# A two-layer token mixer on one core: three weight groups instead of two in the opening of layer 1, and the last convolution moved behind two low parts

## The chip, the core and the metric

One core of a Trainium2 chip runs the whole kernel. The metric is the time of one execution on the device, in microseconds (us). For the kernel before, three timed runs gave 1090.76, 1093.69 and 1093.97 us, median 1093.69. One further execution was recorded by the hardware profiler; all rows shown here are from it.

## The reference

Two layers work on 1024 tokens of width 1024 in fp32. Layer 0 (Fourier mixing beside differential attention, then a gate and an output projection) is not touched by the change, apart from the end of its output projection, where work for layer 1 begins. Layer 1 is a gated short convolution:

```
h = modulate(x, norm_g[1], shift, scale)       # RMS norm per token, then scale and shift
bg, cg, xt, g = split(h @ odd_w_in, 4)         # 1024 -> 4096
u = cg * xt
conv = sum(conv_w[t] * up[:, t:t+n] for t in range(3))   # up is u padded by one token
y = (bg * conv * silu(g)) @ odd_w_out          # 1024 -> 1024
x = x + gate * y
```

## The kernel before

All products are fp32 work on TensorE, done as three matmuls: each factor is split into a high part (a rounded cast) and a low part (value minus high part), and high x high, high x low and low x high are added. The high part is a cast on ScalarE (L61 for weights, L1506 for activations), the low part a subtraction on VectorE or GpSimd (L62, L1309 and L1310 for weights, L1510 for activations).

Layer 1's two projections go by Strassen's scheme in Winograd's form: a block product of 2 x 2 takes seven products of blocks instead of eight. The weights come in 20 groups `g`. Groups 0 to 15 are the input projection, an even `g` giving a tile of `u`, the odd one after it the gated `y`; groups 16 to 19 are the output projection. Each group has seven products `(g, p)`, p = 1 to 7. A product is four `quarters` of three matmuls, 128x512 each, on lines L657 to L659; it needs

- a weight part, made by `wop(g, p)` (L1300) from the raw tiles that `wload(g)` (L1288) fetches by two transfers on SP's queue. p = 1, 2, 3, 4, 6, 7 read a quarter of the raw tiles; p = 5 reads a sum, and `wpart` (L634) makes it and two other sums in place, on GpSimd. A fourth sum, `a_hi -= a_lo`, may be made only once the parts 2 and 5 have read the old values. The argument `held` keeps it for later; `later` makes the cast at once and returns the subtraction as a closure.
- an activation part `B[p]` of four tiles. B1 and B2 are the two token halves. B5, B6, B7, B4 and B3 are sums and differences of them. In layer 1's opening they are built in place from `x1`: `scaled` and `t1` (L1499, L1502) for B5, `shifted` and `t2` (L1516, L1523) for B6, `t3` (by L1502) for B7, `t4` (L1531) for B4, and plain halves for B3, each with `hi` (L1506) and `lo` (L1510).

The products of a group add up in PSUM banks of three kinds: X takes p = 1, 6, 7 and 4 (three buffers), Y p = 5 and 3 (two), Z p = 2 (one). X is read between its products: after (g,1), (g,6), (g,7) and (g,4), while the next of them adds to it.

After a product, `finish1` (L1338) takes what is ready out of the banks: p = 1, 6 and 7 copy X on ScalarE (L1354, L1360, L1363), p = 2 adds Z (L1356), p = 7 adds Y (L1364), p = 4 multiplies by X (L1366), p = 3 adds Y and multiplies (L1371, L1374). After p = 3 of a `u` group the three-tap convolution `conv` runs on VectorE (L1386, L1389). A gated group has a silu besides and ends in the multiplication with the convolution's result `vv`. `finish2` (L1419) does the like for the output projection.

Layer 1 can't scale its second token half before that half's RMS statistics are there: `stats_mid` and `rows_mid` make token sums on TensorE (L209), a root's argument on VectorE (L216), a power on GpSimd (L218), a diagonal `dg` on VectorE (L220) and a row on TensorE (L228). They stand between matmuls of (0,2) and (1,1).

What sets the order: in the opening (the first twelve products, groups 0 and 1) PE, VectorE, ScalarE and GpSimd follow the order in which the code is written, `manual_schedule`. In the middle, up to (13,7), only PE does, and a scheduler places the rest. From (14,1) on all four do again: this is the seam, where groups 14 and 15 end, the output projection's activation parts are built from `ysd` by `bop` (table `hooks`), and the weight parts of groups 16 and on are made, five products ahead (`LEAD`), with their low parts held one product (`rests`, `due`).

Of the kernel before, what the change touches and what calls it, by code (L numbers as in the profile page):

```python
# [37 lines left out]
def block_kernel(tc, A):  # L38
# [1260 lines left out]
    def wop(g, p, eng=None, later=False, held=None):  # L1299

        pool = wpools[0]
        wpools.append(wpools.pop(0))
        rest = []

        def out(src, e):
            o = pool.tile([P, 2, NB], F32R, name="wop", bufs=4 if pool is wp else 2)
# [3 lines left out]
            rest.append(lambda: e.tensor_tensor(out=o[:, 1, :], in0=src, in1=f32(o[:, 0, :]), op=ALU.subtract))  # L1310
# [138 lines left out]
    for half in range(2):  # L1449
        y0(half)  # L1450
        for f in range(KT):
            if half == 0 or f < KT - 1:
# [8 lines left out]
            if half == 1 and f == KT - 1:
                for q in order[:5]:
                    wop(*q)
                man.__exit__(None, None, None)
                man = tc.manual_schedule(engines=MANUAL)
                man.__enter__()
# [238 lines left out]
```

## Time and profile before

| | before |
|---|---|
| median of three runs | 1093.69 us |
| profiled execution | 1093.98 us, span 1092.2 us, mean granted clock of TensorE 0.981 |
| busy: TensorE, VectorE, ScalarE, GpSimd | 1039.5, 753.0, 481.9, 466.8 us |
| HBM read, written | 105.57 MB, 24.64 MB |
| layer 1's first twenty products | 661.10 to 739.50 us of the span |
| the other products of the input projection up to the seam | 739.50 to 985 us |
| the seam and the start of the output projection | 985 to 1030 us |

A row of the trace reads: start, duration, engine, source line, operation, output<-inputs, shapes, count, and in brackets how long the engine stood idle before it and which instruction released it. A row of stages reads: window, length, busy time and instructions of each engine, granted clock as a share of full speed, share of the DMA engines in use, GB/s. A row of waits reads: matmul and line, released by, idle us in all, count, longest. A row of groups reads: line, engine, operation, tiles, shapes, count | busy us, mean ns | idle us before it.

### The profile page before, as it was taken

What the parts mean: (1) busy time and instruction counts of PE and PEld (TensorE: products, weight loads), DVE (VectorE), ACT (ScalarE), POOL (GpSimd) and SP (SyncE); (2) the same over time, 40 slices, a digit from 0 to 9 for tenths busy, and PEclk for the clock granted to TensorE, in tenths of its full rate; (3) what the DMA queues carried; (4) which work ended last, traced back from release to release, by engine and by line L of the source; (5) the groups of instructions that cost most, each with busy time, mean ns of one, the idle gap of its engine ahead of it and who ended that gap; (6) DMA issues with size and microseconds to landing.
All of it is one profiled execution on the core that took longest, in us unless ns stands there. A gap on an engine that the chain in (4) does not pass through costs nothing.

```text
span 1092.2 us, 14128 instructions
## 1 busy us (share of the span) xinstructions
PE 1039.5 (95%) x5128; PEld 847.3 (78%) x5128; DVE 753.0 (69%) x1093; ACT 481.9 (44%) x876; POOL 466.8 (43%) x398
## 2 busy tenths in 40 slices
PE   6989999999999899999999998899999999998998
PEld 3667888878877698999888886578888888786786
DVE  4599956958786388888853287986545645578953
ACT  4453333313345377777753363633333333344420
POOL 1257115620445147766575445655344354402041
PEclk8999999999999999999999999999999999999999
DMA  9823895353112978161006450121111211202431
GB/s 337 329 97 113 260 367 214 110 166 115 59 44 78 244 185 189 38 163 57 11 20 210 166 189 34 38 77 40 59 58 39 77 40 58 77 20 97 143 126 59
DMA packets 61381, 131.12 MB, mean 120 GB/s; under 512 B 5248, under 2 KB 30208, under 8 KB 58112
## 3 DMA queue, kind: packets, MB, share of 16 engines
q1 hardware_dynamic: 60240, 125.64, 36.7%
q0 software_dynamic: 1072, 4.59, 1.2%
q8 instruction: 40, 0.66, 0.2%
q14 instruction: 29, 0.24, 0.1%
HBM read 105.57 MB, written 24.64 MB: 119 GB/s over the span
## 4 chain that ended last, share of the span: by engine, by line
PE 64%; DVE 20%; POOL 5%; ACT 4%; issue 3%; DMA 3%; SPq 0%; ACTq 0%; POOLq 0%; DVEq 0%
PE psX L657 6%; PE psX L659 6%; PE psX L658 6%; PE ps_av L1075 5%; PE ps_tok L284 3%; PE ps_tok L285 3%; PE ps_tok L286 3%; PE psY L657 3%; PE psY L659 3%; PE psY L658 3%; PE S L1025 3%; PE S L1026 2%; DVE nm L1030 2%; PE ps_t L1065 2%; PE ps_feat L1128 2%
## 5 line engine op out<-in xcount | busy, mean ns | idle before, releaser
L284 PE MATMUL ps_tok<-whi,hhi 128*128 128x512 f32 x288 | 118.5, 412 | 2.5 <-ACT hhi L393 1.5
L285 PE MATMUL ps_tok<-whi,hlo 128*128 128x512 f32 x288 | 115.3, 400 | 3.6 <-DVE hlo L397 3.5
L286 PE MATMUL ps_tok<-wlo,hhi 128*128 128x512 f32 x288 | 114.6, 398 | 0.0
L61 ACT CAST wop<-wraw 128x512 fp32r<-128x512 f32 x118 | 72.5, 620 | 93.4 <-PE ps_feat L1130 27.6
L1030 DVE TENSOR_REDUCE nm<-S 128x1 f32<-128x1280 f32 x64 | 95.2, 1487 | 20.5 <-PE S L1026 18.4
L634 POOL TENSOR_TENSOR s<-wraw 128x512 f32<-128x512 f32 x20 | 27.9, 1395 | 185.3 <-DMA wraw<-in_wodd_dram 118.1
L62 POOL TENSOR_TENSOR wop<-wraw,wop 128x512 fp32r<-128x512 f32 x60 | 83.1, 1388 | 51.5 <-ACT wop L61 51.5
L1041 ACT ACTIVATE p<-S,nm 128x1280 f32<-128x1280 f32 x64 | 85.1, 1330 | 43.2 <-DVE nm L1030 39.4
L657 PE MATMUL psX<-B,wop 128*128 128x512 f32 x240 | 96.7, 403 | 7.5 <-ACT c L1363 3.5
L658 PE MATMUL psX<-B,wop 128*128 128x512 f32 x240 | 96.5, 402 | 1.5 <-POOL B L1510 1.0
L659 PE MATMUL psX<-B,wop 128*128 128x512 f32 x240 | 96.1, 401 | 1.8 <-DVE wop L1310 1.3
L1075 PE MATMUL ps_av<-v,aT 128*128 128x128 f32 x640 | 76.8, 275 | 0.0
L1075 PEld LDWEIGHTS ps_av<-v,aT 128*128 128x128 f32 x640 | 74.2, 192 | 0.2
L285 PEld LDWEIGHTS ps_tok<-whi,hlo 128*128 128x128 f32 x288 | 55.5, 193 | 16.9 <-DVE hlo L397 6.0
L659 PE MATMUL psY<-B,wop 128*128 128x512 f32 x160 | 64.3, 402 | 4.1 <-DVE wop L1310 4.1
L284 PEld LDWEIGHTS ps_tok<-whi,hhi 128*128 128x128 f32 x288 | 55.6, 193 | 16.2 <-issue 2.1
L1052 POOL TENSOR_TENSOR p<-p,cc 128x256 f32<-128x256 f32 x32 | 40.3, 1259 | 63.8 <-DVE cc L1049 44.6
L286 PEld LDWEIGHTS ps_tok<-wlo,hhi 128*128 128x128 f32 x288 | 55.4, 192 | 12.2 <-DVE wlo L172 0.2
L658 PE MATMUL psY<-B,wop 128*128 128x512 f32 x160 | 64.1, 401 | 0.6 <-POOL B L1510 0.3
L657 PE MATMUL psY<-B,wop 128*128 128x512 f32 x160 | 64.0, 400 | 0.0
L657 PEld LDWEIGHTS psX<-B,wop 128*128 128x128 f32 x240 | 45.7, 191 | 21.3 <-ACT c L1363 4.8
L658 PEld LDWEIGHTS psX<-B,wop 128*128 128x128 f32 x240 | 45.7, 191 | 14.3 <-POOL B L1510 2.4
(347 smaller groups left out, 2696.0 us busy)
## 6 DMA issues: line engine op xcount, KB each, us to landing
ada_raw<-in_ada_dram SPq DMA_DIRECT2D x24, 1024.0 KB, 7.6
wraw<-in_wodd_dram SPq DMA_DIRECT2D x32, 512.0 KB, 3.5
wraw<-in_wo_dram SPq DMA_DIRECT2D x24, 512.0 KB, 4.1
wraw<-in_wtok_dram SPq DMA_DIRECT2D x16, 512.0 KB, 5.1
arena<-kd SPq DMA_DIRECT2D x16, 320.0 KB, 9.3
kq<-kd SPq DMA_DIRECT2D x16, 320.0 KB, 10.1
xt<-in_xT_dram SPq DMA_DIRECT2D x16, 256.0 KB, 5.8
xr<-in_xT_dram SPq DMA_DIRECT2D x16, 256.0 KB, 4.0
```

The costliest lines, as they stand in the source:

```text
L61: nc.scalar.copy(out=o[:, 0, :], in_=src)
L62: eng.tensor_tensor(out=o[:, 1, :], in0=src, in1=f32(o[:, 0, :]), op=ALU.subtract)
L284: nc.tensor.matmul(ps, lhsT=hh, rhs=whi, start=k == 0, stop=False)
L285: nc.tensor.matmul(ps, lhsT=hl, rhs=whi, start=False, stop=False)
L286: nc.tensor.matmul(ps, lhsT=hh, rhs=wlo, start=False, stop=k == KT - 1)
L657: nc.tensor.matmul(ps, lhsT=a, rhs=x[k][0], start=start and k == 0, stop=False, skip_group_check=not start)
L658: nc.tensor.matmul(ps, lhsT=a, rhs=x[k][1], start=False, stop=False, skip_group_check=not start)
L659: nc.tensor.matmul(ps, lhsT=b, rhs=x[k][0], start=False, stop=k == 3, skip_group_check=not start)
L1030: nc.vector.tensor_reduce(out=nm, in_=S[m][:, :NKEY], op=ALU.max, axis=AX.X, negate=True)
L1041: nc.scalar.activation(out=p, in_=S[m][:, :NKEY], func=AF.Exp, bias=tiles.pop((i, m, "nm")), accum_out=z)
L1052: nc.gpsimd.tensor_tensor(out=p1[:, ks], in0=p1[:, ks], in1=c.broadcast_to([P, POOLK]), op=ALU.mult)
L1075: nc.tensor.matmul(ps, lhsT=groups[i, k // 4][:, (k % 4) * P:(k % 4 + 1) * P], rhs=v[:, k * P:(k + 1) * P], start=k == 0, stop=k == NK - 1)
```

## The change

In words:

- Groups 0, 1 and 2 open layer 1 together, 17 hand-ordered products and three more, instead of groups 0 and 1 with twelve. `order` now begins with six products from B1 and B2.
- Group 0's raw weights go into `w2` and are loaded half a projection earlier; group 2's go into the buffers of `B3` before `B3` is made; two of `B3`'s four tiles go into `x1` buffers.
- All low parts of the opening are made on VectorE; GpSimd has only the weight sums left there. The casts are taken forward (`later=True`) and the subtractions stand where the code names them. The sums `a_hi -= a_lo` of groups 1 and 2 are held, and run on VectorE after (0,4).
- The token sums stand after the first quarter of (0,2) instead of the second.
- `finish1` of (0,3), (1,3) and (14,3) returns its tail, `last`: the convolution or the multiplication with `vv`. For group 14 the tail stands behind the low parts that are due.
- `y` of groups 11 and 13 lies in `B3` buffers; (1,2) uses a Y buffer and (2,5) a buffer of the pool `pst`.

The core of the diff:

```diff
-    wpools[:] = [wp, wp, wp, wp, w2, w2]
+    wpools[:] = [w2, w2, wp, wp, wp, wp]
...
-                pool = (wp, w2)[g % 2]
-                t = pool.tile([P, KT * P], F32, name="wraw", bufs=2)
+                if g == 2:
+                    t = hB.tile([P, KT * P], F32, name="wraw", tag="B3", bufs=4)
+                else:
+                    t = (w2, wp)[(g + (g > 2)) % 2].tile([P, KT * P], F32, name="wraw", bufs=2)
...
-        if p == 3:
-            rest.append(lambda: wload(g + 2))
+        if p == 3 and g != 2:
+            rest.append(lambda: wload(g + 2 + (g < 2)))
...
-            if gated:
+            def last():
+                if not gated:
+                    return conv(ct, ubuf[ct % 2])
+                if g == 1:
+                    nc.vector.tensor_mul(out=h0, in0=h0, in1=vv[:, 0:NB])
                 nc.vector.tensor_mul(out=h1, in0=h1, in1=vv[:, NB:T])
                 ysd.append(us[g])
-            else:
-                conv(ct, ubuf[ct % 2])
+
+            if g in (0, 1, 14):
+                return last
+            last()
...
-    order = [(0, 1), (0, 2), (1, 1), (1, 2), (0, 5), (1, 5), (0, 6), (1, 6), (0, 7), (1, 7), (0, 4), (0, 3)]
-    for g in range(2, 14):
-        order += [(g, 1), (g - 1, 4), (g, 5), (g - 1, 3), (g, 6), (g, 2), (g, 7)]
+    order = [(0, 1), (0, 2), (1, 1), (1, 2), (2, 1), (2, 2), (0, 5), (1, 5), (2, 5), (0, 6), (1, 6), (0, 7), (1, 7),
+             (0, 4), (1, 4), (0, 3), (1, 3), (2, 6), (2, 7), (2, 4)]
+    NMAN = 17
+    for g in range(3, 14):
+        order += [(g, 1)] + [(g - 1, 4)] * (g > 3) + [(g, 5), (g - 1, 3), (g, 6), (g, 2), (g, 7)]
...
-    product(0, 2, (2, stats_mid))
-    wop(1, 6, G)
+    wop(1, 5, V, held=held)
+    product(0, 2, (1, stats_mid))
...
+    w06 = wop(0, 6, V, True)
+    t2(3), lo(6, 2, V)
+    w16 = wop(1, 6, V, True)
+    w06()
+    lo(6, 3, V)
     product(1, 5)
-    shifted(0), shifted(1), t2(0), shifted(2), t2(1), lo(6, 0, V), lo(6, 1, G), shifted(3), t2(2), t2(3), lo(6, 2, V)
-    lo(6, 3, G)
-    wop(0, 7, G)
-    fin12()
-    t3(0), t3(1), lo(7, 0, V), lo(7, 1, G)
+    product(2, 5)
+    t3(0), w16(), t3(1), lo(7, 0, V), t3(2), lo(7, 1, V), t3(3), lo(7, 2, V)
+    w07 = wop(0, 7, V, True)
+    lo(7, 3, V)
     product(0, 6)
...
     product(0, 4)
-    product(0, 3)
+    for f in held:
+        f()
...
-        product(g, p)
+        tail = product(g, p)
         for f in due:
             f()
+        if tail:
+            tail()
```

How this moves rows, at three places. The rows are instructions in the order in which the engine takes them, with line, operation, output<-inputs and size.

First, VectorE between B6 and B7. Tiles `x1` are the activations that are being turned from one part into the next, `wop` with `wraw` is a weight's low part. Before, where only every second low part is here and GpSimd has the others:

```order
L1510 TENSOR_TENSOR B6_6240<-x1_5513,B6_6240 128x512
L1356 TENSOR_TENSOR y_6161<-y_6161,psZ_6184 128x512
L1502 SCALAR_TENSOR_TENSOR x1_5484<-x1_5484,shift1_90,x1_5593 128x512
L1502 SCALAR_TENSOR_TENSOR x1_5498<-x1_5498,shift1_90,x1_5633 128x512
L1510 TENSOR_TENSOR B7_6253<-x1_5484,B7_6253 128x512
L1502 SCALAR_TENSOR_TENSOR x1_5513<-x1_5513,shift1_90,x1_5673 128x512
L1502 SCALAR_TENSOR_TENSOR x1_5553<-x1_5553,shift1_90,x1_5713 128x512
L1510 TENSOR_TENSOR B7_6274<-x1_5513,B7_6274 128x512
```

And in the changed kernel, from the low part of (0,6) to the first step of B4:

```order
L1312 TENSOR_TENSOR wop_6267<-wraw_5851,wop_6267 128x512
L1531 TENSOR_TENSOR B6_6270<-x1_5553,B6_6270 128x512
L1522 SCALAR_TENSOR_TENSOR x1_5484<-x1_5484,shift1_90,x1_5593 128x512
L1312 TENSOR_TENSOR wop_6273<-wraw_5991,wop_6273 128x512
L1522 SCALAR_TENSOR_TENSOR x1_5498<-x1_5498,shift1_90,x1_5633 128x512
L1531 TENSOR_TENSOR B7_6304<-x1_5484,B7_6304 128x512
L1522 SCALAR_TENSOR_TENSOR x1_5513<-x1_5513,shift1_90,x1_5673 128x512
L1531 TENSOR_TENSOR B7_6308<-x1_5498,B7_6308 128x512
L1522 SCALAR_TENSOR_TENSOR x1_5553<-x1_5553,shift1_90,x1_5713 128x512
L1531 TENSOR_TENSOR B7_6312<-x1_5513,B7_6312 128x512
L1531 TENSOR_TENSOR B7_6316<-x1_5553,B7_6316 128x512
L1552 TENSOR_TENSOR x1_5593<-x1_5593,x1_5484 128x512
```

All four low parts of B7, and the weights' low parts of (0,6) and (1,6), now stand in VectorE's row.

Second, ScalarE at the copy of (2,6), `u` from a bank X (L1360 before, L1366 now). The tiles `wraw_6425` before and `wraw_6434` now are raw weights of group 3, `s1` is a weight sum of p = 5. Before:

```order
L61 CAST wop_6468<-wraw_6425 128x512
L61 CAST wop_6484<-wraw_6305 128x512
L61 CAST wop_6507<-s1_6503 128x512
L1373 ACTIVATE y_6162<-y_6162 128x512
L1360 COPY u_6449<-psX_6436 128x512
L61 CAST wop_6523<-wraw_6303 128x512
L61 CAST wop_6544<-wraw_6425 128x512
L1363 COPY c22_6559<-psX_6436 128x512
```

Now:

```order
L1379 ACTIVATE y_6163<-y_6163 128x512
L61 CAST wop_6499<-wraw_6434 128x512
L61 CAST wop_6538<-s1_6534 128x512
L61 CAST wop_6541<-wraw_6085 128x512
L1366 COPY u_6440<-psX_6197 128x512
L1398 ACTIVATE vv_5454<-u_6106,small_76 128x512 x2
L61 CAST wop_6544<-wraw_6434 128x512
L1369 COPY c22_6559<-psX_6197 128x512
```

The casts of group 3 still stand ahead of the copy, but group 3 is now loaded behind the low part of (1,3), and (2,6) and (2,7) follow each other on PE.

Third, VectorE at the seam: the last convolution (taps of 128x256 and less into `vv`) and the low parts of (16,5), `wop` from `s1`, and (17,1). Before:

```order
L1374 TENSOR_TENSOR u_6449<-u_6449,c22_8286 128x512
L1389 SCALAR_TENSOR_TENSOR vv_5454<-u_6449,small_76,vv_5454 128x256 x2
L1389 SCALAR_TENSOR_TENSOR vv_5454<-u_6449,small_76,vv_5454 128x254 x2
L1389 SCALAR_TENSOR_TENSOR vv_5454<-u_6449,small_76,vv_5454 128x255 x2
L1389 SCALAR_TENSOR_TENSOR vv_5454<-u_6449,small_76,vv_5454 128x254 x2
L1389 SCALAR_TENSOR_TENSOR vv_5454<-u_6449,small_76,vv_5454 128x2 x4
L1310 TENSOR_TENSOR wop_8327<-s1_8323,wop_8327 128x512
L1310 TENSOR_TENSOR wop_8354<-wraw_8318,wop_8354 128x512
L1366 TENSOR_TENSOR y_8150<-y_8150,psX_8137 128x512
```

Now:

```order
L1380 TENSOR_TENSOR u_6440<-u_6440,c22_8286 128x512
L1312 TENSOR_TENSOR wop_8327<-s1_8323,wop_8327 128x512
L1401 SCALAR_TENSOR_TENSOR vv_5454<-u_6440,small_76,vv_5454 128x256 x2
L1401 SCALAR_TENSOR_TENSOR vv_5454<-u_6440,small_76,vv_5454 128x254 x2
L1401 SCALAR_TENSOR_TENSOR vv_5454<-u_6440,small_76,vv_5454 128x255 x2
L1401 SCALAR_TENSOR_TENSOR vv_5454<-u_6440,small_76,vv_5454 128x254 x2
L1401 SCALAR_TENSOR_TENSOR vv_5454<-u_6440,small_76,vv_5454 128x2 x4
L1312 TENSOR_TENSOR wop_8354<-wraw_8318,wop_8354 128x512
L1372 TENSOR_TENSOR y_8150<-y_8150,psX_8137 128x512
```

The low part of (16,5) has passed the convolution; that of (17,1) stands where it stood.

More of the change, by code (lines that the diff above doesn't have):

```diff
@@ L1326, in product @@
         if start:
-            banks[g, bank] = pst.tile([P, NB], F32, name="ps" + bank, tag="t", bufs=2) if (g, p) in ((16, 5), (17, 2)) \
+            banks[g, bank] = pst.tile([P, NB], F32, name="ps" + bank, tag="t", bufs=2) \
+                if (g, p) in ((2, 5), (16, 5), (17, 2)) else acc.tile([P, NB], F32, name="psY", bufs=2) if (g, p) == (1, 2) \
                 else acc.tile([P, NB], F32, name="ps" + bank, bufs={"X": 3, "Y": 2, "Z": 1}[bank])
@@ L1332, in product @@
             return lambda: fin(g, p)
-        fin(g, p)
+        return fin(g, p)
     part22 = {}
@@ L1340, in finish1 @@
         X, Y_, Z = (banks.get((g, i)) for i in "XYZ")
+        if p == 5:
+            return
         if p == 1:
@@ L1344, in finish1 @@
             elif gated:
-                us[g] = halves(xp.tile([P, T], F32, name="y", tag="x1", bufs=KT))
+                us[g] = halves(hB.tile([P, T], F32, name="y", tag="B3", bufs=4) if g in (11, 13) else
+                               xp.tile([P, T], F32, name="y", tag="x1", bufs=KT))
             else:
@@ L1366, in finish1 @@
             nc.vector.tensor_tensor(out=h0, in0=h0, in1=X, op=ALU.mult)
-            if gated:
+            if gated and g > 1:
                 nc.vector.tensor_mul(out=h0, in0=h0, in1=vv[:, 0:NB])
@@ L1453, in block_kernel @@
                 w0next()
+            if half == 1 and f == 2:
+                wload(0)
             if half == 1 and f == KT - 2:
-                wload(0)
                 wload(1)
+                man.__exit__(None, None, None)
+                man = tc.manual_schedule(engines=MANUAL)
+                man.__enter__()
             if pend:
@@ L1460, in block_kernel @@
                 ps = proj_feat2(W[half * KT + f], half)
+            if half == 1 and f == KT - 2:
+                wop(0, 1, nc.vector)
+                wop(0, 2, nc.vector)
             if half == 1 and f == KT - 1:
[L1462 to L1466, printed above, removed]
+                wop(1, 1, nc.vector)
+                wop(0, 5, nc.vector)
             out0(half, f, ps)
@@ L1483, in block_kernel @@
     LEAD = 5
-    wop(1, 5)
+    wload(2)
+    wop(1, 2, nc.vector)
     late = {}
+    held = []
     def stats_mid():
@@ L1535, in block_kernel @@
     product(0, 1)
-    wop(0, 6)
-    product(0, 2, (2, stats_mid))
-    wop(1, 6, G)
+    wop(1, 5, V, held=held)
+    product(0, 2, (1, stats_mid))
+    w21 = wop(2, 1, V, True)
+    w22 = wop(2, 2, V, True)
     product(1, 1, (2, rows_mid))
-    scaled(0), scaled(1), t1(0), scaled(2), t1(1), lo(5, 0, V), lo(5, 1, G), scaled(3), t1(2), t1(3), lo(5, 2, V)
-    lo(5, 3, G)
+    w21()
+    w22()
     fin12 = product(1, 2, later=True)
-    product(0, 5)
-    product(1, 5)
-    shifted(0), shifted(1), t2(0), shifted(2), t2(1), lo(6, 0, V), lo(6, 1, G), shifted(3), t2(2), t2(3), lo(6, 2, V)
@@ L1546, in block_kernel @@
-    lo(6, 3, G)
-    wop(0, 7, G)
-    fin12()
-    t3(0), t3(1), lo(7, 0, V), lo(7, 1, G)
+    w25 = wop(2, 5, V, True, held)
+    scaled(0), scaled(1), t1(0), scaled(2), t1(1), lo(5, 0, V), lo(5, 1, V)
+    fin2 = [product(2, p, later=True) for p in (1, 2)]
+    scaled(3), t1(2), t1(3), lo(5, 2, V), lo(5, 3, V)
+    fin12()
+    w25()
+    product(0, 5)
+    shifted(0), shifted(1), t2(0), shifted(2), t2(1), lo(6, 0, V), lo(6, 1, V), shifted(3), t2(2)
+    w06 = wop(0, 6, V, True)
+    t2(3), lo(6, 2, V)
@@ L1550, in block_kernel @@
+    w16 = wop(1, 6, V, True)
+    w06()
+    lo(6, 3, V)
+    product(1, 5)
+    product(2, 5)
+    t3(0), w16(), t3(1), lo(7, 0, V), t3(2), lo(7, 1, V), t3(3), lo(7, 2, V)
+    w07 = wop(0, 7, V, True)
+    lo(7, 3, V)
     product(0, 6)
-    t3(2), t3(3), lo(7, 2, V), lo(7, 3, G)
-    wop(1, 7, G)
+    t4(0), w07(), t4(1), lo(4, 0, V)
+    w17 = wop(1, 7, V, True)
     product(1, 6)
-    wop(0, 4, G)
-    wop(0, 3, G)
-    t4(0), t4(1), lo(4, 0, V), lo(4, 1, G), t4(2), t4(3), lo(4, 2, V), lo(4, 3, V)
+    t4(2), lo(4, 1, V), t4(3), w17(), lo(4, 2, V)
@@ L1557, in block_kernel @@
+    w04 = wop(0, 4, V, True)
+    lo(4, 3, V)
     product(0, 7)
-    hi(3, 0), hi(3, 1), lo(3, 0, V), lo(3, 1, G), hi(3, 2), hi(3, 3), lo(3, 2, V), lo(3, 3, G)
+    w04()
+    hi(3, 0), hi(3, 1)
+    w14 = wop(1, 4, V, True)
+    lo(3, 0, V), hi(3, 2), lo(3, 1, V), hi(3, 3), w14(), lo(3, 2, V)
     product(1, 7)
-    wop(2, 1)
+    w03 = wop(0, 3, V, True)
+    lo(3, 3, V)
     product(0, 4)
-    product(0, 3)
+    for f in held:
+        f()
+    w03()
+    w13 = wop(1, 3, V, True)
+    for f in fin2:
+        f()
@@ L1563, in block_kernel @@
+    w13()
+    product(1, 4)
+    w26 = wop(2, 6, V, True)
+    w27 = wop(2, 7, V, True)
+    w26()
+    w27()
+    tails = [product(0, 3)]
+    wop(2, 4, V)
+    tails.append(product(1, 3))
+    wop(3, 1, V)
+    product(2, 6)
+    for f in tails:
+        f()
     man.__exit__(None, None, None)
@@ L1573, in block_kernel @@
     for n, (g, p) in enumerate(order):
-        if n < 12:
+        if n <= NMAN:
             continue
```

6 lines of the change are left out of this document (3 added, 3 removed).

## The prediction

> **What bounds the kernel now.** I read the page first, then the busy time by stage, then what TensorE waited for in the stages that lose time, then single rows there.
>
> ```profile
> span 1092.2 us, 14128 instructions
> PE 1039.5 (95%) x5128; PEld 847.3 (78%) x5128; DVE 753.0 (69%) x1093; ACT 481.9 (44%) x876; POOL 466.8 (43%) x398
> ...
> core 0: us, PE busy (x) PEld busy (x) DVE busy (x) ACT busy (x) POOL busy (x), PEclk, DMA share, GB/s
> 661.10:739.50 78.40, 66.62 (x260) 49.36 (x259) 67.88 (x79) 35.09 (x61) 47.81 (x33) 0.93 0.13 44
> 739.50:985.00 245.50, 245.29 (x1052) 196.76 (x1051) 137.20 (x224) 93.93 (x159) 94.44 (x68) 1.00 0.17 54
> 985.00:1030.00 45.00, 38.15 (x148) 29.02 (x147) 42.30 (x67) 20.39 (x37) 8.62 (x6) 0.92 0.29 92
> ```
>
> TensorE is the bound, and the change neither adds nor removes a matmul, so only its idle time and its slowed clock can be won. Between 739.50 and 985 it never rests: nothing is to be had there. Two stages lose time at a clock below 1: the opening of layer 1 (661.10 to 739.50) and the seam to the output projection (985 to 1030). In both VectorE is nearly full, 67.88 of 78.40 and 42.30 of 45.
>
> ```profile
> 661.10 0.40 PE L657 MATMUL psX<-arena,wop 128*128 128x512 f32 x1
> 665.30 0.28 PE L209 MATMUL ps_ss<-ones,x1ss 128*128 128x1 f32 x2
> 667.00 0.48 PE L657 MATMUL psZ<-arena,wop 128*128 128x512 f32 x1
> 673.71 1.44 PE L228 MATMUL ps_r<-dg,ones 128*128 128x512 f32 x2 [3.67 <-DVE dg L220]
> 674.27 1.30 PE L657 MATMUL psX<-arena,wop 128*128 128x512 f32 x1
> 705.64 0.79 PE L657 MATMUL psX<-B,wop 128*128 128x512 f32 x1 [2.46 <-ACT c L1363]
> 707.08 0.63 PE L657 MATMUL psX<-B,wop 128*128 128x512 f32 x1
> 707.51 0.63 PE L658 MATMUL psX<-B,wop 128*128 128x512 f32 x1
> 732.25 0.67 PE L657 MATMUL psX<-B,wop 128*128 128x512 f32 x1 [2.65 <-ACT u L1360]
> 736.70 0.40 PE L657 MATMUL psX<-arena,wop 128*128 128x512 f32 x1
> 739.50 0.40 PE L657 MATMUL psX<-B,wop 128*128 128x512 f32 x1
> 992.96 0.50 PE L657 MATMUL psX<-B,wop 128*128 128x512 f32 x1 [0.84 <-ACT c L1363]
> ```
>
> One product (12 matmuls) takes 739.50 - 736.70 = 2.80 us at full clock. The first twenty products of layer 1 end at 739.50; undisturbed they are 56.0 us, and they took 78.4: 22.4 lost. Of this the token sums (667.00 - 665.30 = 1.7) and the row of statistics (674.27 - 673.71 = 0.6) are work. The other 20.1 are three long waits (3.67, 2.46, 2.65), the matmuls behind each, which start 0.43 apart (707.51 - 707.08) instead of 2.80/12 = 0.23, and small waits for VectorE's and GpSimd's low parts.
>
> **The change in the opening.** Before, twelve products stand against the building of the activation parts; now twenty do. TensorE gets six products from the first two activation parts (six against four) before it needs VectorE's next one, then three, two, two, two, two.
>
> The statistics:
>
> ```profile
> 657.49 1.76 POOL L634 TENSOR_TENSOR s<-wraw 128x512 f32<-128x512 f32 x1 [4.74 <-DMA wraw<-in_wodd_dram]
> 668.93 1.77 DVE L62 TENSOR_TENSOR wop<-wraw,wop 128x512 fp32r<-128x512 f32 x1 [1.30 <-ACT wop L61]
> 670.86 1.02 POOL L218 TENSOR_TENSOR rs<-rs,mhalf 128x4 f32<-128x4 f32 x1 [0.70 <-DVE rs L216]
> 671.91 1.75 DVE L220 TENSOR_TENSOR dg<-cst,rs 128x512 f32<-128x512 f32 x1 [1.13 <-POOL rs L218]
> ```
>
> The token sums ended at 667.0, but a weight's low part (668.93 to 670.7) stood ahead of the root on VectorE. That part hangs on GpSimd's sums, which began at 657.49 with group 0's. In the new order group 0's four sums stand far ahead, among GpSimd's low parts in layer 0's output projection, so group 1's come first and I put that part ready at about 666.5; and the token sums stand three matmuls sooner. My chain: sums end 666.3, root on VectorE 667.2, power 1.0, `dg` 1.75 as now, row 670.5. TensorE has nine and six matmuls (3.5) until 669.9: it waits 0.7, not 3.67. VectorE's first `scaled` comes at 673.0, behind two low parts for group 2, against 675.19.
>
> VectorE's pace (first row: the stretch from the first scaling step to the last `B3` part, VectorE busy and its instructions):
>
> ```profile
> 675.19:710.20 35.01, 34.11 (x38) 0.91 0.09 30
> 675.19 1.41 DVE L1499 SCALAR_TENSOR_TENSOR x<-x,sc,ps_r 128x512 f32<-128x512 f32 x2 [0.94 <-PE ps_r L228]
> 685.98 0.68 DVE L1510 TENSOR_TENSOR B<-x,B 128x512 fp32r<-128x512 f32 x1
> 686.58 0.74 DVE L1499 SCALAR_TENSOR_TENSOR x<-x,sc,ps_r 128x512 f32<-128x512 f32 x1
> 687.24 2.01 DVE L1523 TENSOR_TENSOR x<-x,x 128x512 f32<-128x512 f32 x2
> 706.70 2.99 POOL L1510 TENSOR_TENSOR B<-x,B 128x512 fp32r<-128x512 f32 x2 [1.13 <-ACT B L1506]
> 707.25 3.00 DVE L1510 TENSOR_TENSOR B<-x,B 128x512 fp32r<-128x512 f32 x2
> 685.50 0.73 ACT L1516 ACTIVATE x<-x,shift 128x512 f32<-128x512 f32 x1
> 686.13 0.61 ACT L1506 CAST B<-x 128x512 fp32r<-128x512 f32 x1
> ```
>
> Alone, a low part takes 686.58 - 685.98 = 0.60 and a scaling step 687.24 - 686.58 = 0.66; beside GpSimd two low parts take 3.00. The change takes GpSimd out of this stretch, so VectorE inherits nine low parts of B and five of weights but runs at 0.60 and 0.66. Ends of the change's cost for a low part moved over: 0.60 and 1.50 each; I take 0.60, since GpSimd's queue holds only the sums of groups 2 and 3 now. The two held sums cost VectorE 2 x 0.60 late, where TensorE has work.
>
> The walk along VectorE's queue from 673.0: 26 instructions (12 of 0.66, 14 of 0.60: 16.3) and an estimated 1.5 of gaps for ScalarE's shifts and casts (0.73 and 0.61 each) up to the low part of (0,6): 690.8. Twelve more (7.4) to that of (0,7): 698.2. Six more (3.6) to that of (1,7): 701.8. TensorE reaches (0,5) at 661.1 + 6 x 2.8 + 1.7 + 0.7 + 0.6 = 680.9 and needs the low part of (0,6), its third matmul, at 680.9 + 8.4 + 0.5 = 689.8: it waits 1.1. Two products on, 696.5 against 698.2: 1.7. One product on, 701.1 against 701.8: 0.7. After that VectorE is ahead.
>
> New waits: (2,6), (2,7) and (2,4) now follow each other in one bank, so each copy by ScalarE stands open; the nearest row, the 0.84 wait at 992.96, prices one at 0.9. The first is worse: on ScalarE the copy stands behind the cast of group 3's sum, which needs a load that SP issues behind VectorE's low part of (1,3).
>
> ```profile
> wraw<-in_wodd_dram SPq DMA_DIRECT2D x10, 512.0 KB, 3.6
> ```
>
> I put the issue at 712.2 (third of a burst), the landing at 716.2, GpSimd's sum 1.3, two casts, the copy at 719.6: TensorE, ready at 718.1, waits 1.6. Ends: 0.9, and 5 if the load lands late.
>
> Sum of waits: 0.7 + 1.1 + 1.7 + 0.7 + 1.6 + 0.9 = 6.7. For slowed matmuls behind them the ends are 0.1 each (behind the 0.84 wait the next matmul is late by that) and 1.5 each (2.46: six or seven matmuls, 0.2 each). Three of mine lie at 1.1 to 1.7, nearer the first: 1.0 in all. The twenty products end at 661.1 + 56.0 + 2.3 + 6.7 + 1.0 = 727.1, against 739.5: **12.4 us won**.
>
> The Trainium skill (TensorE: Matmul & The Clock Gate, Part 1) lets the clock fall only after an idle window of about 3.4 us. By it none of my waits would slow a matmul, and the result would be 1.0 lower; the trace disagrees, since waits of 2.46 and 2.65 did.
>
> ```profile
> L62 POOL TENSOR_TENSOR wop<-wraw,wop 128x512 fp32r<-128x512 f32 x26 | 36.1, 1392 | 37.3 <-ACT wop L61 37.3
> ```
>
> Costed at nothing: group 0's four early sums during the output projection of layer 0 (the row is 560 to 661: GpSimd idles 37.3/26 = 1.4 before each low part, so four sums of about 1.3 are caught up within four parts; without that cover TensorE would wait up to 5.2 there); group 2's raw weights in the `B3` buffers; two `B3` parts in `x1` slots, free by then.
>
> **The change at the seam.**
>
> ```profile
> PE psY L659 <- DVE wop L1310: 4.1, 1, 4.1
> PE psX L659 <- DVE wop L1310: 1.3, 2, 0.8
> ...
> 1001.10 4.40 DVE L1389 SCALAR_TENSOR_TENSOR vv<-u,small,vv 128x256 f32<-128x256 f32 x12
> 1005.42 0.69 DVE L1310 TENSOR_TENSOR wop<-s,wop 128x512 fp32r<-128x512 f32 x1
> ...
> 1006.34 1.51 POOL L634 TENSOR_TENSOR s<-wraw 128x512 f32<-128x512 f32 x1 [10.03 <-DVE wop L1310]
> 1009.62 1.28 POOL L634 TENSOR_TENSOR wraw<-s,wraw 128x512 f32<-128x512 f32 x1
> ...
> L1389 DVE SCALAR_TENSOR_TENSOR vv<-u,small,vv 128x254 f32<-128x254 f32 x4 | 4.0, 996 | 0.0
> ```
>
> Only the low part of (16,5) passes the last convolution; that of (17,1) stays behind it. The 4.1 wait goes, and (17,1) waits instead. VectorE is full until its low part of (17,6), the last that TensorE waits for, so its work decides. That frees GpSimd's sums for (17,5) to run beside the convolution (4.4 us, 1006.34 to 1010.9), whose taps then take about 1.0 instead of 4.40/12 (0.48 the large ones): +2.2, less the 1.4 by which the same sums slow VectorE's steps now: about +0.5 with the rest. The last `B3` casts now wait for low parts that read `y` of groups 11 and 13: one gap of 0.8. Ends: -2.6 (the 4.1 and the small waits gone) to +2.5; I take **1.3 lost**.
>
> By the Trainium skill (SBUF — State Buffer, two separate sides) a GpSimd instruction and a VectorE one with two SBUF inputs exclude each other for whole instructions. By that the convolution would grow by all of 4.4 and the time would be 2.2 higher; the rows, 996 ns a tap beside GpSimd, say about half.
>
> **Sum.** 12.4 - 1.3 = 11.1. The profiled execution took 1093.98 outside a span of 1092.2; it gives 1082.9. The median of the runs is 0.3 lower, 1093.69: **1082.6**.
>
> **Rivals.**
> - TensorE bound throughout: VectorE starts and runs a little better, and no low part is late. Then 56.0 + 2.3 and perhaps 1 of waits, about 18 won: 1075 (with the seam's best 1072). For it: my three VectorE waits are under 2 us. Against: VectorE's 54 instructions from `scaled` to the last `B3` part are 33.5 at the bare pace, so a wait of some kind stays.
> - The third group's chain gives half back: the load for group 3, or ScalarE's queue behind the silu of group 1, holds (2,7) for 5 to 6 with the clock behind it, as 2.65 at 732.25 did. Then 5 to 6 won: 1088.
> - Nothing won: after the opening VectorE has two convolutions in a row, TensorE catches up with it and the opening's gain is waited off there: 1091 to 1095. Against it: VectorE is 137.20 of 245.50 in the next stage.
> - Slower: VectorE's slowness isn't GpSimd's doing. From 675.19 to 710.20 it ran 38 instructions in 35.01, 0.92 each. At that pace the 54 take 49.7 instead of 33.5 + 1.5 = 35.0: 14.7 later, against 11.1 won, and with the clock behind the waits 1098. It decides from (35.0 + 11.1)/54 = 0.85 an instruction. Against it: the slow rows all lie beside GpSimd rows.
>
> **How the numbers follow.** The forecast 0.60 (own range 1079.5 to 1086), TensorE bound 0.14, half given back 0.14, nothing won 0.07, slower 0.05. The runs before lie within 0.3% of each other, about what a measurement can tell. Faster by more is 0.60 + 0.14 + 0.14 = 0.88, within it 0.07, slower 0.05. The range 1076 to 1089 leaves out half of the first rival, and of the others nothing won and slower.
>
> **What would show it.** In the profile after: the wait for `dg` under 1.5; no GpSimd row of B; low parts of B at 0.69; the first twenty products in 64 to 69 us; waits for weights' low parts at (0,6) and (0,7), and for ScalarE's copy at (2,7). At the seam: the wait of 4.1 at (17,1) instead of (16,5), taps near 1.0. Wrong would be a wait over 3 us in the opening, or low parts of B still over 1 us.

## The result, and the profile after

The changed kernel takes 1081.25 us, median of three runs (1080.91 to 1082.07), against 1093.69: a ratio of 0.9902, 95% interval 0.9879 to 0.9926, so 1% faster. Run twice more among the experiments, on two chips, it gave 0.9908 (0.9891 to 0.9925) and 0.9913 (0.9899 to 0.9928), 9.5 to 9.8 us under the medians of before there. The forecast was 1082.6.

The profiled execution took 1081.25 outside a span of 1079.4. By stage (window, length, busy time of TensorE, its weight loads, VectorE, ScalarE and GpSimd, then the clock), first of before and then of the changed kernel. The opening of before stands in the prediction, so its rows begin with the stretch from the end of the twentieth product to the start of (14,1); the last row of each is the seam, counted here and below from the start of (14,1), at 952.30 in before, to the start of (18,1):

```profile
739.50:952.30 212.80, 212.80 (x914) 170.94 (x913) 115.86 (x190) 78.46 (x131) 90.57 (x65) 1.00 0.17 55
952.30:1047.72 95.42, 88.36 (x361) 69.07 (x360) 76.83 (x119) 39.49 (x70) 18.95 (x13) 0.96 0.32 103
```

```profile
658.83:722.71 63.88, 59.94 (x259) 46.67 (x258) 58.08 (x86) 34.69 (x61) 15.46 (x11) 1.00 0.13 39
722.71:935.56 212.85, 212.85 (x914) 171.11 (x913) 124.34 (x201) 77.84 (x131) 89.49 (x64) 1.00 0.17 55
935.56:1034.69 99.13, 88.59 (x362) 68.72 (x360) 79.73 (x119) 39.80 (x70) 18.01 (x13) 0.97 0.31 102
```

The reader is to see three differences. The first twenty products take 63.88 instead of 78.40 (14.5 won), at full clock, and GpSimd is busy 15.46 there instead of 47.81. The middle is unchanged. The seam takes 99.13 instead of 95.42 (3.7 lost). A fourth lies ahead of all changed work: layer 1 begins at 658.83 instead of 661.10. 2.27 + 14.52 - 0.05 - 3.71 = 13.0, which is the span's 12.8 but for the last stretch.

What TensorE still waits for in the two stages (released by, idle us in all, count, longest), the opening first, then the seam:

```profile
PE psX L657 <- ACT u L1366: 2.5, 2, 1.3
PE psX L659 <- DVE wop L1312: 0.7, 2, 0.6
PE psX L657 <- ACT c L1369: 0.7, 1, 0.7
...
PE psX L659 <- DVE wop L1312: 7.4, 3, 3.8
PE psY L658 <- DVE B L1259: 1.7, 1, 1.7
PE psX L657 <- ACT c L1369: 0.9, 2, 0.7
PE psZ L659 <- DVE wop L1312: 0.6, 1, 0.6
```

In the opening the longest wait is 1.32, and the wait for `dg` is gone. In the seam the 4.1 has become a 3.8; two waits for weights' low parts have grown, at (16,6) from 0.60 to 2.06 and at (17,6) from 0.75 to 1.51; and one for `B3`, ahead of (16,3), has come. The rows:

```profile
665.51 1.78 DVE L220 TENSOR_TENSOR dg<-cst,rs 128x512 f32<-128x512 f32 x1 [1.13 <-POOL rs L218]
667.62 1.02 PE L228 MATMUL ps_r<-dg,ones 128*128 128x512 f32 x2
693.74 0.50 PE L657 MATMUL psX<-B,wop 128*128 128x512 f32 x1 [1.32 <-ACT u L1366]
716.07 0.50 PE L657 MATMUL psX<-B,wop 128*128 128x512 f32 x1 [1.20 <-ACT u L1366]
984.77 6.34 DVE L1401 SCALAR_TENSOR_TENSOR vv<-u,small,vv 128x256 f32<-128x256 f32 x12
985.08 1.31 POOL L634 TENSOR_TENSOR s<-wraw 128x512 f32<-128x512 f32 x1 [5.72 <-ACT vv L1398]
986.47 1.35 POOL L634 TENSOR_TENSOR wraw<-wraw 128x512 f32<-128x512 f32 x1
991.76 0.80 PE L659 MATMUL psX<-arena,wop 128*128 128x512 f32 x1 [3.79 <-DVE wop L1312]
1005.25 0.50 PE L659 MATMUL psX<-B,wop 128*128 128x512 f32 x1 [2.06 <-DVE wop L1312]
1012.15 0.69 DVE L1259 TENSOR_TENSOR B<-y,B 128x512 fp32r<-128x512 f32 x1 [0.69 <-ACT B L1274]
1013.50 0.50 PE L659 MATMUL psX<-B,wop 128*128 128x512 f32 x1 [1.51 <-DVE wop L1312]
1028.52 0.50 PE L658 MATMUL psY<-B,wop 128*128 128x512 f32 x1 [1.71 <-DVE B L1259]
```

The diagonal ends at 667.29, 0.3 before TensorE takes it. The convolution's twelve taps now take 6.34 instead of 4.40, and the two rows of GpSimd lie beside them. The 0.69 is the gap for a `B3` cast.

### The profile page after: what moved, and what is told of

Its sections match the earlier page's. It is cut to its first block, busy times and chain, and to the rows that moved or that the text cites. A ratio compares the mean times of both kernels' runs of the same rounds, so it can differ in the third digit from the quotient of the medians.

```text
span 1079.4 us, 14123 instructions
## 1 busy us (share of the span) xinstructions
PE 1031.8 (96%) x5128; PEld 843.3 (78%) x5128; DVE 760.0 (70%) x1112; ACT 480.7 (45%) x876; POOL 436.8 (40%) x379
## 4 chain that ended last, share of the span: by engine, by line
PE 64%; DVE 21%; POOL 4%; ACT 4%; issue 3%; DMA 3%; SPq 0%; ACTq 0%; POOLq 0%; DVEq 0%
PE psX L657 6%; PE psX L659 6%; PE psX L658 6%; PE ps_av L1075 5%; PE ps_tok L284 3%; PE ps_tok L285 3%; PE ps_tok L286 3%; PE psY L658 3%; PE psY L659 3%; PE psY L657 3%; PE S L1025 3%; PE S L1026 3%; DVE nm L1030 2%; PE ps_t L1065 2%; DMA ada_raw<-in_ada_dram 2%
## 5 line engine op out<-in xcount | busy, mean ns | idle before, releaser
L1030 DVE TENSOR_REDUCE nm<-S 128x1 f32<-128x1280 f32 x64 | 95.2, 1487 | 22.0 <-PE S L1026 17.2
L61 ACT CAST wop<-wraw 128x512 fp32r<-128x512 f32 x106 | 65.2, 619 | 82.7 <-PE ps_feat L1130 22.0
L657 PE MATMUL psX<-B,wop 128*128 128x512 f32 x240 | 95.6, 398 | 5.0 <-ACT u L1366 2.5
L659 PE MATMUL psX<-B,wop 128*128 128x512 f32 x240 | 95.3, 397 | 4.3 <-DVE wop L1312 4.3
L658 PE MATMUL psX<-B,wop 128*128 128x512 f32 x240 | 94.8, 395 | 0.0
L62 POOL TENSOR_TENSOR wop<-wraw,wop 128x512 fp32r<-128x512 f32 x52 | 71.5, 1377 | 42.1 <-ACT wop L61 42.0
```

Source lines behind the costliest of these rows:

```text
L62: eng.tensor_tensor(out=o[:, 1, :], in0=src, in1=f32(o[:, 0, :]), op=ALU.subtract)
L657: nc.tensor.matmul(ps, lhsT=a, rhs=x[k][0], start=start and k == 0, stop=False, skip_group_check=not start)
L658: nc.tensor.matmul(ps, lhsT=a, rhs=x[k][1], start=False, stop=False, skip_group_check=not start)
L659: nc.tensor.matmul(ps, lhsT=b, rhs=x[k][0], start=False, stop=k == 3, skip_group_check=not start)
L1030: nc.vector.tensor_reduce(out=nm, in_=S[m][:, :NKEY], op=ALU.max, axis=AX.X, negate=True)
```

## The experiments

Single executions of one kernel differ by 3 us and more (1077.95 to 1084.6 for the changed one on one chip), so single terms are read from the stages of the profiles; times stand beside them.

**The changed kernel again.**

> The changed kernel once more, as the base for the others. In its first profile layer 1 began 2.27 us earlier than in the profile of before, though nothing that runs up to there differs but four weight sums on GpSimd. Theory: that 2.27 is where TensorE's clock happens to fall in the first 30 us, so the start of layer 1 lies at 658 to 662 from run to run, while the stretch from it to the end of the twentieth product stays at 63.9 +- 0.3 and the time at 1080 to 1083. Rival: it belongs to the change; then the start is again at 658.8 +- 0.4.

1081.0 us. Layer 1 began at 659.22; twenty products took 66.47, the seam 97.13. Over all 13 profiles taken, the start lay between 657.48 and 661.79; in the two others that have the opening of before (`seam_alone`, `two_groups_vector` below) it lay at 659.00 and 660.10, and the 3430 matmuls ahead of it stand in the same order in all. So the 2.27 is no part of the change, as the theory said. That TensorE's clock in the first 37 us makes it is shown for a part only. Here is that clock, in before and then in the changed kernel's first profile:

```profile
5.00:37.00 32.00, 26.18 (x117) 15.33 (x118) 16.07 (x34) 14.35 (x30) 6.96 (x6) 0.83 0.94 361
```

```profile
5.00:37.00 32.00, 26.38 (x120) 15.47 (x121) 17.76 (x37) 14.56 (x31) 6.95 (x6) 0.92 0.99 374
```

The 430th of those matmuls starts at 111.50 in before and at 110.24 in the other, so 1.26 of the 2.27 is there by then; the rest comes between there and 417 us. Over all profiles this clock does not decide the start: 0.79 went with 659.00, 0.83 with 658.63, 0.95 with 660.38. What does stays open.

The opening missed the theory: 66.47 instead of 63.9. The wait at (2,7) was 2.27 instead of 1.20, with a stretch at half clock behind it. The rows ahead of the copy in this run, and the clock behind it:

```profile
710.61 1.29 POOL L634 TENSOR_TENSOR s<-wraw 128x512 f32<-128x512 f32 x1 [39.49 <-DMA wraw<-in_wodd_dram]
710.71 1.74 DVE L1380 TENSOR_TENSOR u<-u,c 128x512 f32<-128x512 f32 x1
712.37 1.79 DVE L62 TENSOR_TENSOR wop<-wraw,wop 128x512 fp32r<-128x512 f32 x1
714.08 0.68 DVE L1377 TENSOR_TENSOR y<-y,psY 128x512 f32<-128x512 f32 x1
714.79 0.63 ACT L1379 ACTIVATE y<-y 128x512 f32<-128x512 f32 x1 [6.28 <-DVE y L1377]
716.88 0.57 ACT L1366 COPY u<-psX 128x512 f32<-128x512 f32 x1
717.50 0.50 PE L657 MATMUL psX<-B,wop 128*128 128x512 f32 x1 [2.27 <-ACT u L1366]
```

```profile
718.40:721.80 3.40, 3.40 (x10) 2.42 (x8) 3.37 (x4) 0.80 (x2) 3.04 (x3) 0.50 0.00 0
```

The copy stands behind ScalarE's silu of group 1, that behind VectorE's addition, and that behind two VectorE instructions slowed by GpSimd's sums for group 3. In the first profile the sum began 0.24 later against layer 1's start (710.46 at 658.83, here 710.61 at 659.22), and only one of the two was slowed:

```profile
710.34 0.69 DVE L1380 TENSOR_TENSOR u<-u,c 128x512 f32<-128x512 f32 x1
710.46 1.72 POOL L634 TENSOR_TENSOR s<-wraw 128x512 f32<-128x512 f32 x1 [39.72 <-DVE u L1377]
```

What decides is which of the two starts first. In all ten profiles with the new opening the first kept its own time (0.69 for L1380, 1.29 for the sum), and the other took 1.66 to 1.83. The sum was first in three, by 0.04 to 0.17, and where the three products follow each other as here, TensorE then waited 1.88 to 2.31 at (2,7), against 1.20 or 1.21 in the others.

**The seam alone.** The kernel before, with only this:

```diff
-        fin(g, p)
+        return fin(g, p)
...
-            else:
+            elif g == 14:
+                return lambda: conv(ct, ubuf[ct % 2])
+            else:
                 conv(ct, ubuf[ct % 2])
...
-        product(g, p)
+        tail = product(g, p)
         for f in due:
             f()
+        if tail:
+            tail()
```

> The kernel before with only the last convolution put behind the low parts that are due; its opening is untouched. Theory (VectorE decides in the seam, and GpSimd's sums of group 17 now run beside the taps): the wait of 4.1 moves from (16,5) to (17,1), the twelve taps take 6.3 instead of 4.4, VectorE's low part of (17,5) comes 1.2 later, and the kernel is 1 to 2 us slower than before. Rival (the low part behind the convolution was what bound, so its wait goes): 2 to 4 us faster.

1092.55 us against 1090.81, ratio 1.0014 (1.0003 to 1.0024). The seam took 96.72 instead of 95.42: 1.3 lost, and in the time 0.3 to 2.6, as the theory had it.

```profile
998.42 6.34 DVE L1391 SCALAR_TENSOR_TENSOR vv<-u,small,vv 128x256 f32<-128x256 f32 x12
998.73 1.31 POOL L634 TENSOR_TENSOR s<-wraw 128x512 f32<-128x512 f32 x1 [5.71 <-ACT vv L1388]
1000.12 1.36 POOL L634 TENSOR_TENSOR wraw<-wraw 128x512 f32<-128x512 f32 x1
1005.42 0.80 PE L659 MATMUL psX<-arena,wop 128*128 128x512 f32 x1 [3.81 <-DVE wop L1310]
```

The wait has moved to (17,1), and 2.67 of GpSimd beside the taps cost VectorE 6.34 - 4.40 = 1.94.

**The opening alone.**

```diff
-            if g in (0, 1, 14):
+            if g in (0, 1):
```

> The changed kernel with the last convolution where it was before, ahead of the low parts; the new opening stays. Theory: taps 4.4 again, waits at (16,6), (17,2), (17,6) down to about 1.4, 0.6, 1.5 (the gap for the B3 cast stays), 1.0 to 2.0 us faster than the changed kernel, 13 to 15 faster than before. Rival (the 4.0 lost in the seam come from where y and the weights lie now, not from the convolution): within 0.5 of the changed kernel.

1080.78 us, ratio 0.9911 (0.9890 to 0.9932), beside 1081.0 of the changed kernel on the same chip: in the time, nothing that can be told. The seam took 96.64, against 99.13, 97.13 and 97.26 in the three profiles of the changed kernel. Most of that spread is the one wait for `B3` ahead of (16,3): 0.50 here, 1.71, none and none there. Without it the seam takes 96.1 here and 97.1 to 97.4 there, so the convolution's place costs about 1, the low end of the theory (a table of all profiles stands at the end of this section). What is left against the 95.42 of before can't be the convolution's place.

**B4 later.**

```diff
-             (16, 1): [(7, 3, 4), (4, 0, 2)], (16, 5): [(4, 2, 4)], (17, 1): [(3, 0, 4)]}
+             (16, 1): [(7, 3, 4)], (17, 5): [(4, 0, 2)], (16, 2): [(4, 2, 4)], (16, 6): [(3, 0, 4)]}
```

> The changed kernel, with the building of B4 put behind (17,5) and (16,2) instead of (16,1) and (16,5), and B3 behind (16,6) instead of (17,1): twelve VectorE instructions of 0.6 (7 us) move behind the low parts of (16,6), (17,2) and (17,6). Theory (VectorE's order decides there, and B4 is needed only at the eleventh product): the waits of 2.06, 0.61 and 1.51 go, 3 to 4.2 us faster than the changed kernel. Rival (VectorE is simply full through the seam, the waits return at (16,7) to (16,3)): 0 to 1 faster.

1081.33 us, the seam 99.78: no gain. The rival held. The three waits did go, and these came:

```profile
1016.18 0.47 PE L657 MATMUL psX<-B,wop 128*128 128x512 f32 x1 [1.05 <-DVE u L1431]
1021.89 0.47 PE L657 MATMUL psX<-B,wop 128*128 128x512 f32 x1 [2.67 <-DVE out L1431]
1033.23 0.50 PE L658 MATMUL psY<-B,wop 128*128 128x512 f32 x1 [1.64 <-DVE B L1259]
```

The last of them, for `B3`, was there in the first profile too (1.71). The work that was put off stands in front of the additions (L1431) that empty the banks. VectorE is full through the seam, so its order only chooses where TensorE waits.

**Low parts back on GpSimd.** The changed kernel, with `lo(5, 1, V)`, `lo(5, 3, V)` and seven like them as `G`.

> The changed kernel with the nine activation low parts of the opening that GpSimd had before back on GpSimd (every second one of B5, B6, B7 and B3, one of B4). Theory (beside GpSimd VectorE slows by as much as it is spared): VectorE has 45 instructions instead of 54 up to the last B3 part, but at about 0.85 to 0.92 instead of 0.64 each, so that part comes 3 to 6 us later and the first twenty products take 66 to 70 us instead of 63.9 to 66.5. Rival (GpSimd's help is real help): VectorE is done 5 us earlier, the waits at (0,7) and (1,7) go, 62 to 64 us.

1085.43 us, ratio 0.9936 (0.9916 to 0.9956). The first 17 products of layer 1 take 55.45 instead of 53.07, the twenty 66.26. VectorE's stretch from the first scaling step to the low part of `B3`'s third tile, in the changed kernel and then here, and GpSimd's nine here:

```profile
669.51:703.04 33.53, 32.92 (x54) 1.00 0.04 12
```

```profile
672.47:708.98 36.51, 36.27 (x46) 0.95 0.05 14
```

```profile
L1531 POOL TENSOR_TENSOR B<-x,B 128x512 fp32r<-128x512 f32 x9 | 13.1, 1453 | 21.1 <-ACT B L1527 21.1
```

54 instructions at 0.62 against 46 at 0.79: with eight fewer VectorE needs 3.0 longer. The theory holds, at the low end of its size (its pace was to be 0.85 to 0.92).

**Two groups, all on VectorE.** The kernel before, with its fourteen `G` of the opening as `V`.

> The kernel before with all fourteen low parts that GpSimd had in the opening (nine of activations, five of weights) on VectorE; two groups open, as before. Theory (the third group's six products are the cover, the low parts only make them enough): VectorE has 14 more instructions at 0.64 instead of 0.92, no earlier end; the first twenty products take 74 to 78 us, 0 to 3 us faster than before. Rival (the low parts alone carry the gain): 66 to 70 us, 8 to 11 us faster.

1090.79 us, ratio 0.9985 (0.9969 to 1.0002): nothing that the time can tell. Twenty products took 75.50, against 78.40 in before and 77.10 in `seam_alone`, which has the same opening as before: 1.6 to 2.9 less. But the first twelve, where the moved parts lie, took 51.55, against 51.54 and 52.37. Most of what was won lies behind them, with the wait at (2,7), which was 1.30 instead of 2.65 and 2.07. So the low parts' move alone wins 0 to 0.8 where it is made.

With nine of the fourteen back on GpSimd (the run before) the rest of the new opening still wins 78.40 - 66.26 = 12.1. That is not all the third group's. 5.5 of it lie in (1,1) and (1,2), which took 11.95 in before with the wait for `dg` and the slowed matmuls behind it, and 6.44 in both kernels with the new opening; the third group's products stand behind these two and can't cover them. About 6.6 is left for its six products and the rest of the order; no run parts these.

**(2,6), (2,7) and (2,4) apart.** With the convolution ahead of the low parts, and weight casts two products less ahead just there:

```diff
-    for g in range(3, 14):
...
+    order[-2:] = [(3, 1), (2, 7), (3, 5), (2, 4), (2, 3), (3, 6), (3, 2), (3, 7)]
+    for g in range(4, 14):
...
-        while wn < min(n + LEAD + 1, len(order)):
+        while wn < min(n + LEAD + 1 - 2 * (n <= 22), len(order)):
```

> The changed kernel with the last convolution ahead of the low parts again, and with (2,6), (2,7), (2,4) no longer back to back in one bank: (2,6), (3,1), (2,7), (3,5), (2,4), (2,3). Theory (each of the three copies by ScalarE stands open only because the next product wants the bank at once): the waits of 1.2 to 2.3 and 0.7 there go, with the slowed clock behind them; from the start of layer 1 to the end of the first 22 products 1.7 to 4 us less than the same 22 take there now, 1078 to 1079 us in all. Rival (group 3's load is what is late, so (3,1) waits instead): the same wait at (3,1), no gain.

1084.91 us, ratio 0.9928 (0.9900 to 0.9956). The first 22 products took 67.39, against 69.48 in the changed kernel's first profile and 70.85 in `opening_alone`: the waits went. But the rest of the input projection lost 6:

```profile
735.28 0.72 ACT L1398 ACTIVATE vv<-u,small 128x512 f32<-128x512 f32 x1 [5.52 <-DVE u L1372]
739.60 0.72 ACT L1398 ACTIVATE vv<-u,small 128x512 f32<-128x512 f32 x1 [3.09 <-DVE u L1380]
740.23 0.57 ACT L1366 COPY y<-psX 128x512 f32<-128x512 f32 x1
740.85 0.80 PE L657 MATMUL psX<-B,wop 128*128 128x512 f32 x1 [3.35 <-ACT y L1366]
```

```profile
739.50:746.30 6.80, 5.45 (x13) 4.29 (x14) 4.01 (x12) 2.87 (x5) 0.00 (x0) 0.50 0.24 77
```

TensorE comes to (3,7) 2.0 sooner after layer 1's start than in the changed kernel's first profile, where the copy of (3,6) ended just as TensorE came. Here that copy stands on ScalarE behind the second convolution's start and ends 1.3 later; ahead of it two VectorE steps (L1385 and L1386) met GpSimd's low parts and took 1.75 and 1.78 instead of 0.68. Neither the theory nor the rival had that. By this profile the waits at (2,7) and (2,4) are worth little by themselves: without them TensorE runs into VectorE here.

**Token sums later.** `product(0, 2, (2, stats_mid))` in the changed kernel.

> The changed kernel with the token sums after the second quarter of (0,2), as before, instead of after the first. Theory (the sums are 0.7 later, the row dg had 0.3 to spare, and everything VectorE builds hangs on it): a wait of 0.3 to 0.6 for dg, and the first 17 products of layer 1 take 0.5 to 1.0 more than the 53.07 of the changed kernel; so of the 3.67 that TensorE waited for dg before, the moved sums are under 1, and the weight's low part that stood ahead of the root is the rest. Rival (the moved sums are what took the wait away): 2 to 3 more.

1082.93 us, ratio 0.9927 (0.9906 to 0.9948). The first 17 products took 53.75: 0.68 more, with a wait of 0.26 for `dg`, just under the 0.3 to 0.6 expected. The theory holds: of the 3.67 the earlier sums are under 1. That the rest is the weight's low part is read from the rows; no run puts that part back.

**The y of groups 9 and 11.** With the convolution ahead of the low parts:

```diff
-                us[g] = halves(hB.tile([P, T], F32, name="y", tag="B3", bufs=4) if g in (11, 13) else
+                us[g] = halves(hB.tile([P, T], F32, name="y", tag="B3", bufs=4) if g in (9, 11) else
...
+        if (g, p) == (17, 7):
+            low()
```

> The changed kernel with the last convolution ahead of the low parts again, the y of groups 9 and 11 instead of 11 and 13 in the B3 buffers, and the last low part of the output projection's B3 made behind (17,7) instead of ahead of (16,3). Theory (two B3 casts wait for low parts that read the y whose buffers they take; with groups 9 and 11 those low parts come one earlier): VectorE's gap of 0.69 there shrinks to 0.3 or less, the wait at (17,6) goes from 1.52 to 0.8 to 1.1, the one for B ahead of (16,3), 0.5 to 1.7, is gone, and from (14,1) to (18,1) it takes 95.4 to 96.2 instead of 96.64. Rival (the gap is not from these buffers): 96.6 or more.

1078.34 us, ratio 0.9878 (0.9856 to 0.9900), the seam 95.21. Then beside the changed kernel on one chip:

> The changed kernel a third time, as the base for the next one on the same chip: 0.988 to 0.992 of before. Layer 1's start is again anywhere from 657 to 662, its first 17 products take 53.0 to 53.1.

> The version with the last convolution ahead of the low parts, y of groups 9 and 11 in the B3 buffers and the last B3 low part behind (17,7), beside the changed kernel on one chip. Theory (2 to 3.9 us less between (14,1) and (18,1), nothing else): 95.2 +- 0.3 there, 2 to 4 us faster than the changed kernel. Rival (its first result was the luck of its runs): within 1 us of it.

1081.83 us, 0.9913 (0.9899 to 0.9928), for the changed kernel, whose 17 products took 53.06 (53.07 in its first profile), and 1078.29, 0.9876 (0.9860 to 0.9893), for this version: 3.5 us faster, so it beats both. The seam, 97.26 there, takes 95.47 here:

```profile
935.72:1031.19 95.47, 88.13 (x361) 68.97 (x360) 77.54 (x119) 39.68 (x70) 18.83 (x13) 0.96 0.31 102
```

```profile
PE psY L659 <- DVE wop L1312: 4.1, 1, 4.1
PE psX L659 <- DVE wop L1312: 1.7, 2, 0.9
PE psX L657 <- ACT c L1369: 1.0, 2, 0.8
PE psZ L659 <- DVE wop L1312: 0.6, 1, 0.6
```

Against `opening_alone` the wait at (17,6) is 0.9 instead of 1.5, the 0.69 gap of VectorE is gone, and so is the wait for `B3`. The stage gives 1.8, a little under the 2 that the theory asked for. The two profiled executions differ by 3.2, and 1.4 of that lies ahead of layer 1 (it began at 658.99 and 660.38), which is luck of the start; so of the 3.5 between the medians the traces explain about 1.8.

The seam in all profiles but that of `b4_later`, in us:

| seam | profiles | (14,1) to (18,1) | wait for `B3` in it | without that wait |
|---|---|---|---|---|
| of before | before, `two_groups_vector` | 95.42, 95.99 | 0, 0.49 | 95.4, 95.5 |
| of before, convolution later | `seam_alone` | 96.72 | 0 | 96.7 |
| of the changed kernel | its three, `lows_gpsimd`, `sums_later` | 99.13, 97.13, 97.26, 97.23, 97.79 | 1.71, 0, 0, 0, 0.49 | 97.4, 97.1, 97.3, 97.2, 97.3 |
| the same, convolution earlier | `opening_alone`, `interleave` | 96.64, 97.91 | 0.50, 1.58 | 96.1, 96.3 |
| the last, with this edit | `y_9_11` twice | 95.21, 95.47 | 0, 0 | 95.2, 95.5 |

So the convolution's later place costs 0.8 to 1.3, the buffers of `y` (with the last low part's place) 0.6 to 1.1, and the wait for `B3` 0 to 1.7 from run to run. Slowed matmuls cost nothing here: `y_9_11` had 3.4 us at half clock and then a wait of 1.87 at (16,6), its second run 6.8 us and 0.78, and the stage took as long. TensorE comes later and waits less, since VectorE sets the pace.

## Why the prediction was right, and where it was not

The mechanism was right: VectorE without GpSimd beside it, more products in front of it, and a wait in the seam that moves. That the time came out within 1.35 of the forecast is in part luck. The 2.27 by which layer 1 began sooner in the profile is no part of the change, and the two large terms missed against each other: 12.4 in the opening was 14.5, and 1.3 in the seam was 3.7 in the first profile (1.7 and 1.8 in the other two). Without the start that profile gives 14.5 - 3.7 = 10.8 against 11.1 forecast, and the medians of the later runs give 9.5 to 9.8. Single profiles can't price the opening closer than a few us: before took 78.40 and 77.10, the changed kernel 63.88 and 66.47, so 10.6 to 14.5 was won.

- **dg.** Forecast 0.7 of wait, measured none, with 0.3 to spare. The steps were right, but the root came 5.4 after layer 1's start instead of 6.1. `sums_later` prices the earlier sums at 0.68; by the rows the rest is the low part of (0,6), which no longer stands ahead of the root.
- **VectorE's pace.** 0.60 and 0.66 an instruction was right (0.62 measured). The 1.5 for ScalarE's casts was too much, and its start came 10.7 after layer 1's instead of 11.9, so the low part of (0,6) was no wait at all (1.1 forecast). At (0,7) the 1.7 was about right in size and had another cause in front: 1.32 for ScalarE's copy of (0,6), which stands behind casts of B7 that wait for VectorE's steps, and only then 0.19 for the low part. At (1,7) it was 0.56 against 0.7.
- **(2,7).** 1.6 forecast, 1.20 to 2.27 measured in the changed kernel, by another chain than the one named: not the cast that needs the load, but GpSimd's sum beside VectorE, then the silu. (2,4): 0.9 forecast, 0.68 measured.
- **Slowed matmuls.** 1.0 forecast; none in the changed kernel's first profile, and a stretch of 3.4 at half clock in the next, behind the 2.27.
- **The seam.** The wait moved to (17,1) as forecast, and the gap for the `B3` casts was 0.69 against 0.8. The taps grew by 1.94 against 2.2, which was right by two errors: half of 4.4 of GpSimd's sums was forecast, while only 2.67 ran beside them, the third sum coming behind VectorE's low part of (17,1), and each us of those cost 0.73. All in all the convolution's place cost 0.8 to 1.3 where about 0.5 was forecast. One step was left out: `B3`'s last low part stands behind two weights' low parts, and if GpSimd's first sum for group 18 starts before these, as in the first profile, the two take 3.33 instead of 1.28. That was worth 0 to 1.7 from run to run, and 0.49 once with the seam of before. `y_9_11` removes it and the gap, and the seam is then what it was before.
- **The rivals.** Slower at 0.92 an instruction: it would have needed GpSimd's slowing to be VectorE's own, and `lows_gpsimd` shows it comes with GpSimd. TensorE bound throughout: no, the first profile's 63.88 is 5.6 over the undisturbed 58.3, and 3.9 of that is waits. The third group's chain: it is the mechanism of the 66.47 run, with 2.27 of wait instead of 5 to 6. Nothing won, by two convolutions in a row: not here, but `interleave` shows that it stands right behind.

On the Trainium skill's rule that a VectorE instruction with two SBUF inputs and a GpSimd one exclude each other (SBUF — State Buffer, two separate sides), these runs show more than the half that was taken. That half was misread: the four taps of 996 ns on average are two that met GpSimd, 1.51 each, and two that did not, 0.48 each. In the changed kernel's first profile, too, only two of the twelve taps met a sum. They took 1.39 and 1.51 instead of 0.48, each to 0.28 or 0.29 after its sum's end; the other ten took what they took before. So the one that starts second waits for the first to end, as at (2,7). By these rows the rule holds.

## What to carry to other kernels

When TensorE waits at the head of a stage, look for matmuls whose operands are ready before the slow engine's first output, and for work that needn't stand ahead of what TensorE waits for: here the first was worth up to about 6.6, the second, with the earlier token sums, about 5.5. Moving low parts from GpSimd to VectorE was worth 2.4 with three groups (55.45 against 53.07) and 0 to 0.8 in the first twelve products with two. Two engines that slow each other are no two engines: count a helper by what it costs the one it helps. And where one engine is full through a stage, changing its order only moves the wait; look for what its instructions themselves wait for, such as a buffer whose last reader comes late.

## What the runs showed of the hardware that was not expected

TensorE's clock fell to 0.50 for stretches of 3.4 or 6.8 us. In the profiles of this study every wait of TensorE over 2.3 us in layer 1 had such a stretch at its end or right behind it. One stretch came behind less, a wait of 1.32 and one of 0.19 (`opening_alone`). Of the waits between 1.9 and 2.3 some had one and some had not: at one product of the seam, in the three profiles of the changed kernel, waits of 2.05 and 2.05 had, 2.06 had not. TensorE: Matmul & The Clock Gate, Part 1, of the Trainium skill says that the clock is set by a window of about 3.4 us that runs free of the kernel. The stretches' lengths agree with that, and so does the chance in it; that a whole window has to be idle does not.
